# The final normalisation of an encoder trunk: half of its products given to GpSimd

## Chip, cores and metric

The kernel runs on one core of a Trainium2 chip. The metric is the time of one execution on the device in microseconds (us), as a median of several runs. Five engines work side by side on a core and meet by semaphores: TensorE (PE; PEld is its weight load), VectorE (DVE), ScalarE (ACT), GpSimd (POOL) and SyncE (SP), which here only issues transfers. An engine name with a q behind it is the engine's sequencer, which issues DMAs. The profile comes from one execution recorded by the hardware.

## What is computed

The reference is a trunk of two layers on 512 tokens of 1024 channels. Each layer adds a token mixer and then a gated feed-forward block to the residual stream x, and at the end stands an RMS norm with a gain for each channel:

```python
def rmsnorm(x, g):
    xf = x.astype(jnp.float32)
    y = xf * lax.rsqrt(jnp.mean(xf * xf, axis=-1, keepdims=True) + EPS)
    return (y * g.astype(jnp.float32)).astype(x.dtype)

def conv_ffn(h, w_up, conv_w, conv_b, w_down):
    u, v = jnp.split(h @ w_up, 2, axis=-1)
    u = causal_dwconv(u, conv_w, conv_b)
    return (jax.nn.gelu(u, approximate=False) * v) @ w_down

# in reference(), for each layer l:
        x = x + y                                   # the mixer
        x = x + conv_ffn(rmsnorm(x, ffn_norm[l]), ...)
    return rmsnorm(x, final_norm)
```

The change lies wholly in the last line, the final norm, and in what feeds it.

## The kernel before

The residual stream lies transposed in SBUF: channels on the 128 partitions, tokens along the row. `xall` holds eight tiles `x[0]` to `x[7]`, tile k with channels 128k to 128k+127 and 512 tokens; `x3` is the same memory seen as (partition, tile, token). All products with weights are done in three parts (high times high, high times low, low times high) to keep float32 accuracy. The page's L538 and L268 are these matmuls, L490 and L227 the splitting of weights into parts.

Order. In `ffn` (line 616) every step is put on a plan with a time worked out by hand (`at`), sorted, and traced in that order; `run_plan` (line 436) then holds TensorE, VectorE and ScalarE to it (`planned`, line 433). GpSimd and SP are not in that set: the framework orders what they issue, by what is ready and by the order in the program. DMAs that ScalarE issues stand in ScalarE's planned order.

The last down projection of the second layer (`halves_last`, lines 843 and 875 to 882) is cut in two halves of 256 tokens, so that the first half can be finished while TensorE works on the second. Each half is six groups of seven matmuls; in the second half a counter moves on behind each third of an `accumulate` (`tick`, line 252), and `after(n, fn)` (line 249) runs `fn` when the counter has moved n times. So the small matmuls of the first half's norm stand between the second half's groups.

For every tile j the plan calls `last(j)` (line 1463) when `x[j]` is final. For a whole tile (j from 0 to 6) it squares `x[j]` on ScalarE, adds the square to `acc` on VectorE (`square_acc`, line 288) and, for j up to 5, multiplies `x[j]` in place by the norm's gain on ScalarE (L1471). `x[7]` comes in halves: `last(7, 0)` and `last(7, 1)`. For a half of the tokens, these steps follow:

- the square of `x[7]`'s half on ScalarE (L1474);
- `one`: matmuls with a column of ones sum `acc` and the square over the channels, so that the sum for token t lies on partition t (L1481, bank `ss` of PSUM), and `rsqrt_small` (line 296) makes the root's reciprocal of 128x2 numbers: v = sum/width + eps on VectorE (L298), a first guess y on ScalarE straight from the sum (L300), and a Newton step t = y v, t = -t y / 2, y (t + 1.5) on VectorE (L304 to L306);
- `two`: `spread_small` (line 329) spreads the factor over all partitions with two matmuls against the identity (L332), into a bank `bc` of PSUM;
- `scale_out` (line 1501): for each pair of tiles k = 0, 2, 4, 6, VectorE multiplies the pair's half by the factor, read from PSUM. Pairs 0, 2 and 4 take one product of 128x512 (L1505); the pair 6 takes two operations of 128x256 (L1508), which also multiply by the gain. Then one DMA of 256 KB takes the pair's half to DRAM (L1511). In the first half all four are issued by SP, in the second pairs 2 and 6 by ScalarE.

The first half's `one` runs after two ticks and its `two` after four; its `scale_out` is traced only in `last(7, 1)`, behind the second half's residual sum (`add_x`, L814 and L815): pairs 0 and 2 first, pair 4 between the second half's guess y and its Newton step, pair 6 behind the step. The second half's `scale_out` ends the kernel.

Of the kernel before, what the change touches and what calls it, by code (L numbers as in the profile page):

```python
# [7 lines left out]
F32 = mybir.dt.float32  # L8
F32R = mybir.dt.float32r
I32 = mybir.dt.int32  # L10
AF = mybir.ActivationFunctionType
ALU = mybir.AluOpType

P = 128
T = 512
D = 1024
KD = D // P
# [7 lines left out]
EPS = 1e-6  # L25
# [48 lines left out]
def trunk_kernel(ctx, tc, xT, cols, w_ab, w_pool, w_abo, w_vg, w_qk, w_r, w_g2, w_go, w_up, w_dn, w_ds, outT):  # L74
    nc = tc.nc
    V, S, G, PE = nc.vector, nc.scalar, nc.gpsimd, nc.tensor
# [6 lines left out]
    sp = ctx.enter_context(tc.tile_pool(name="sp", bufs=2))  # L83
    ps = ctx.enter_context(tc.tile_pool(name="ps", bufs=8, space=bass.MemoryType.PSUM))

    def slot(dt=F32, name="s"):
        return big.tile([P, T], dt, tag="s", name=name)
# [17 lines left out]
    def bank(name="ps"):  # L105
        return ps.tile([P, T], F32, tag="ps", name=name)
# [3 lines left out]
    x = [xall[:, k * T : (k + 1) * T] for k in range(KD)]  # L110
# [4 lines left out]
    def col(name, i=0):  # L115
        c = COLS[name] + i
        return colt[:, c : c + 1]
# [45 lines left out]
    eps_t = cp.tile([P, 1], F32, tag="eps", name="eps_t")  # L163
# [85 lines left out]
    def after(n, fn):  # L249
        pending.append((done[0] + n, fn))  # L250
# [9 lines left out]
    def accumulate(out, wh, wl, ah, al, first=True, last=True, step=None, cut=0, loose=False):  # L260
        n = len(ah)
        if cut:
            accumulate(out, wh, wl, ah[:cut], al[:cut], first, False)
            accumulate(out, wh[:, cut:, :], wl[:, cut:, :], ah[cut:], al[cut:], False, last)
            return
        for i, (w, a) in enumerate(((wh, ah), (wh, al), (wl, ah))):
            for k in range(n):
                PE.matmul(  # L268
                    out, w[:, k, :], a[k], start=first and i == 0 and k == 0, stop=last and i == 2 and k == n - 1,
                    skip_group_check=loose,  # L270
                )
            if step:
                step()
# [14 lines left out]
    def square_acc(k, acc, ts=slice(0, T)):  # L288
        if k == 0 and ts.start == 0:
            S.activation(acc[:, ts], x[0][:, ts], AF.Square)  # L290
            return
        sq = slot(name="sq")
        S.activation(sq[:, ts], x[k][:, ts], AF.Square)
        V.tensor_tensor(acc[:, ts], acc[:, ts], sq[:, ts], ALU.add)

    def rsqrt_small(dst, ssum, n, width, between=None):
        v = sp.tile([P, n], F32, tag=f"v{n}", name="v")
        V.tensor_scalar(v, ssum, 1.0 / width, EPS, ALU.mult, ALU.add)  # L298
        y = sp.tile([P, n], F32, tag=f"y{n}", name="y")
        S.activation(y, ssum, AF.Abs_reciprocal_sqrt, bias=eps_t, scale=1.0 / width)  # L300
        if between:
            between()
        t = sp.tile([P, n], F32, tag=f"t{n}", name="t")
        V.tensor_tensor(t, y, v, ALU.mult)  # L304
        V.scalar_tensor_tensor(t, t, -0.5, y, ALU.mult, ALU.mult)
        V.scalar_tensor_tensor(dst, t, 1.5, y, ALU.add, ALU.mult)  # L306
# [22 lines left out]
    def spread_small(y, n):  # L329
        b = bank("bc")[:, : n * P]  # L330
        for c in range(n):
            PE.matmul(  # L332
                b[:, c * P : (c + 1) * P], y[:, c : c + 1].broadcast_to([P, P]), ident, start=True, stop=True
            )
        return b
# [32 lines left out]
    def scaled(o, rs, tag):  # L368
        u = slot(name=tag)
        V.tensor_tensor(u, o, rs, ALU.mult)  # L370
        return u
# [177 lines left out]
    def mix_out(name, gname, acc, lead, fetched):  # L549
# [6 lines left out]
        def part(n, ks, first, last):  # L556
            if first:
                o[n] = (bank(name), *ready.pop(0))
            out, h, lo = o[n]
            accumulate(out, h[:, ks, :], lo[:, ks, :], y_h[ks], y_l[ks], first, last, loose=True)  # L560
# [420 lines left out]
    for j in range(4):  # L981
# [7 lines left out]
        b = scaled(pb, rs, "v")  # L989
# [6 lines left out]
    total = []  # L996
# [272 lines left out]
    t = 0.0  # L1269
# [193 lines left out]
    def last(j, half=None):  # L1463
        if not squares:
            squares.append(slot(name="acc"))
        acc = squares[0]
        ts = slice(0, T) if half is None else slice(half * 256, half * 256 + 256)
        if half is None:
            square_acc(j, acc)
            if j < KD - 2:  # L1470
                S.activation(x[j], x[j], AF.Copy, scale=col("fin", j))  # L1471
            return
        sq = slot(name="sq")[:, :256]
        S.activation(sq, x[j][:, ts], AF.Square)  # L1474
        y2 = sp.tile([P, 2], F32, tag="y2", name="y2")

        def one(between=None):
            b = bank("ss")
            for i, t in enumerate((acc[:, ts], sq)):
                for c in range(2):  # L1480
                    PE.matmul(  # L1481
                        b[:, c : c + 1], t[:, c * P : (c + 1) * P], ones[:, 0:1],
                        start=i == 0 and c == 0, stop=i == 1, skip_group_check=True,
                    )
            rsqrt_small(y2, b[:, :2], 2, D, between)

        def two():
            return ts, spread_small(y2, 2)

        if half:  # L1490
            scale_out(*spread[0], (0, 2))
            one(lambda: scale_out(*spread[0], (4,)))
            scale_out(*spread[0], (6,))
            scale_out(*two(), range(0, KD, 2))
        else:
            after(2, one)
            after(4, lambda: spread.append(two()))

    spread = []

    def scale_out(ts, b, ks):
        for k in ks:
            o3 = x3[:, k : k + 2, ts]
            if k < KD - 2:
                V.tensor_tensor(o3, o3, b[:, None, :].broadcast_to([P, 2, 256]), ALU.mult)  # L1505
            else:
                for i in range(2):
                    V.scalar_tensor_tensor(  # L1508
                        x[k + i][:, ts], x[k + i][:, ts], col("fin", k + i), b, ALU.mult, ALU.mult
                    )  # L1510
            (nc.scalar if k % 4 and ts.start else nc.sync).dma_start(  # L1511
                outT[k * P : (k + 2) * P, ts].rearrange("(a p) t -> p a t", p=P), o3
            )
# [78 lines left out]
```

## Time and profile before

| | |
|---|---|
| median of 3 runs | 1006.32 us (1005.56 to 1007.13) |
| the profiled execution, time | 1006.93 us |
| its span | 1005.2 us, mean TensorE clock 0.997 |
| TensorE busy | 994.8 us, 99% of the span |
| VectorE, ScalarE, GpSimd busy | 851.2, 615.8, 81.3 us |
| HBM read, written | 145.35 MB, 2.10 MB |

How to read the profile's rows. In a timeline a row gives the start in us, the time in us, engine, line of the kernel, operation, output and inputs by tile names, shapes and how many; behind it in brackets, how long the engine was idle before and what released it. A group's row gives the total busy time and the mean in ns behind the bar. The chain is followed back from the last instruction, each step to what released it. A row of stretches gives for each engine its busy time and number of instructions, then TensorE's granted clock, the busy share of the 16 DMA engines and the rate in GB/s. DMA issues are not counted as busy time of the issuing engine. Times on GpSimd are rough.

### The profile page before, as it was taken

The numbers are of one execution on the slowest core, as the hardware profiler recorded it, in microseconds if no ns is written. First come the engines' busy times: TensorE is split into PE (matmuls) and PEld (weight loads), VectorE is DVE, ScalarE is ACT, GpSimd is POOL, SyncE is SP. The second block draws the span as 40 slices with busy tenths as digits, with TensorE's granted clock in tenths as the row PEclk, the third lists the DMA queues.
The fourth block names the chain that finished last, engine by engine and source line by source line (L and its number), as shares of the span: only waits on it lengthen the run. The fifth ranks groups of instructions, "written<-read, shape, count | busy, mean of one in ns | idle before, by whom it ended". The sixth has DMA issues, their size and how long they took to land.

```text
span 1005.2 us, 17757 instructions
## 1 busy us (share of the span) xinstructions
PE 994.8 (99%) x7070; PEld 927.9 (92%) x7070; DVE 851.2 (85%) x1241; ACT 615.8 (61%) x959; POOL 81.3 (8%) x105
## 2 busy tenths in 40 slices
PE   9999999999999999999999999999999999999996
PEld 7888889999999988899999998889999999988896
DVE  7886689999999997768768788889999999997775
ACT  6442467666766764445785677667766666754451
POOL 0000111111101000002000000111101101000000
PEclk9999999999999999999999999999999999999998
DMA  6523757787687454527326122676788777454522
GB/s 224 156 97 105 181 123 185 193 210 191 190 208 181 129 134 132 140 85 198 108 76 145 53 67 93 185 171 165 213 207 194 195 202 188 127 128 142 129 86 84
DMA packets 64083, 151.22 MB, mean 150 GB/s; under 512 B 5408, under 2 KB 8352, under 8 KB 64000
## 3 DMA queue, kind: packets, MB, share of 16 engines
q1 hardware_dynamic: 46640, 117.46, 37.8%
q0 software_dynamic: 16672, 31.99, 19.2%
q8 instruction: 55, 0.90, 0.3%
q10 hardware_dynamic: 688, 0.65, 0.2%
q14 instruction: 28, 0.23, 0.1%
HBM read 145.35 MB, written 2.10 MB: 147 GB/s over the span
## 4 chain that ended last, share of the span: by engine, by line
PE 91%; DVE 4%; DMA 2%; ACT 1%; issue 1%; DVEq 0%; ACTq 0%
PE stx L538 27%; PE styz L538 16%; PE dn L268 15%; PE r L1323 4%; PE abo L268 4%; PE go L268 4%; PE pc L268 2%; PE dn L538 2%; PE px L268 2%; PE pb L268 2%; DMA raw<-in_w_up 2%; PE stz L538 2%; PE vg L1111 1%; PE vg L1113 1%; PE vg L1112 1%; PE pu L268 1%
## 5 line engine op out<-in xcount | busy, mean ns | idle before, releaser
L490 DVE TENSOR_TENSOR lo<-raw,hi 128x1024 fp32r<-128x1024 f32 x112 | 136.7, 1221 | 14.1 <-ACT hi L484 13.8
L484 ACT ACTIVATE hi<-raw 128x1024 fp32r<-128x1024 f32 x112 | 117.8, 1057 | 33.2 <-DMA raw<-in_w_up 12.8
L227 DVE TENSOR_TENSOR lo<-raw,hi 128x1024 fp32r<-128x1024 f32 (+3 forms) x79 | 91.1, 1155 | 18.2 <-ACT hi L223 17.7
L466 POOL DMA_DIRECT2D s<-in_w_up x44 | 53.1, 1206 | 530.1 <-ACT yh L177 97.3
L223 ACT ACTIVATE hi<-raw 128x1024 fp32r<-128x1024 f32 (+3 forms) x79 | 78.7, 997 | 13.2 <-DMA raw<-in_w_ab 4.7
L359 DVE SCALAR_TENSOR_TENSOR cacc<-u,colt,cacc 128x511 f32<-128x511 f32 x96 | 71.5, 745 | 3.9 <-ACT cacc L356 3.8
L356 ACT ACTIVATE cacc<-u,colt 128x512 f32<-128x512 f32 x48 | 39.2, 817 | 49.5 <-DVE u L660 39.9
L490 DVE TENSOR_TENSOR lo<-s,hi 128x1024 fp32r<-128x1024 f32 x56 | 68.2, 1217 | 0.0
L538 PE MATMUL stx<-th,hi 128*128 128x256 f32 x384 | 59.4, 277 | 0.3 <-ACT kk L645 0.3
L484 ACT ACTIVATE hi<-s 128x1024 fp32r<-128x1024 f32 x56 | 59.0, 1053 | 0.7
L538 PE MATMUL stx<-th,lo 128*128 128x256 f32 x384 | 59.1, 276 | 0.0
L538 PE MATMUL stx<-tl,hi 128*128 128x256 f32 x384 | 59.1, 276 | 0.0
L538 PE MATMUL styz<-xl,hi 128*128 128x256 f32 x368 | 57.2, 277 | 0.3
L538 PE MATMUL styz<-xh,hi 128*128 128x256 f32 x368 | 56.9, 277 | 0.0
L538 PE MATMUL styz<-xh,lo 128*128 128x256 f32 x368 | 56.7, 276 | 0.0
L268 PE MATMUL dn<-mh,hi 128*128 128x512 f32 (+1 forms) x238 | 56.5, 377 | 0.0
L268 PE MATMUL dn<-mh,lo 128*128 128x512 f32 (+1 forms) x238 | 56.4, 376 | 0.0
L268 PE MATMUL dn<-ml,hi 128*128 128x512 f32 (+1 forms) x238 | 56.4, 376 | 0.0
L538 PEld LDWEIGHTS stx<-th,hi 128*128 128x128 f32 x384 | 50.7, 188 | 0.7 <-ACT kk L645 0.7
L538 PEld LDWEIGHTS stx<-tl,hi 128*128 128x128 f32 x384 | 50.7, 188 | 0.0
L538 PEld LDWEIGHTS stx<-th,lo 128*128 128x128 f32 x384 | 50.7, 188 | 0.0
L268 PEld LDWEIGHTS dn<-ml,hi 128*128 128x128 f32 x238 | 42.9, 188 | 8.2
(334 smaller groups left out, 2583.3 us busy)
## 6 DMA issues: line engine op xcount, KB each, us to landing
s<-in_w_up SPq DMA_DIRECT2D x44, 512.0 KB, 6.9
s<-in_w_up POOLq DMA_DIRECT2D x44, 512.0 KB, 7.3
raw<-in_w_up SPq DMA_DIRECT2D x44, 512.0 KB, 6.7
raw<-in_w_dn SPq DMA_DIRECT2D x32, 448.0 KB, 3.4
raw<-in_w_up SPq DMA_DIRECT2D x44, 256.0 KB, 3.6
raw<-in_w_ab SPq DMA_DIRECT2D x14, 512.0 KB, 3.6
raw<-in_w_abo SPq DMA_DIRECT2D x8, 512.0 KB, 3.6
s<-in_w_ds SPq DMA_DIRECT2D x8, 512.0 KB, 6.9
```

The source lines that it names most:

```text
L223: S.activation(parts[0], raw, AF.Copy)
L227: V.tensor_tensor(parts[1], raw, f32(parts[0]), ALU.subtract)
L268: PE.matmul(out, w[:, k, :], a[k], start=first and i == 0 and k == 0, stop=last and i == 2 and k == n - 1, skip_group_check=loose,)
L356: S.activation(acc[0], u, AF.Identity, bias=col(bname, j), scale=col(wname, 2 * nj + j))
L359: V.scalar_tensor_tensor(a, u[:, : T - i], col(wname, (2 - i) * nj + j), a, ALU.mult, ALU.add)
L466: G.dma_start(w["s31"].rearrange("p (a n) -> p a n", a=2), part, accum_op=ALU.add)
L484: S.activation(h, src(), AF.Copy)
L490: V.tensor_tensor(lo, src(), f32(h), ALU.subtract)
L538: PE.matmul(b[out][:, ts], wt[:, ks[k]], a[k], start=first and i == 0 and k == 0, stop=i == 2 and k == HK - 1, skip_group_check=True,)
L1111: PE.matmul(o[c][:, :n], xh[kk][:, cs], h[:, k, :], start=kk == 0, stop=False)
L1112: PE.matmul(o[c][:, :n], xl[kk][:, cs], h[:, k, :], start=False, stop=False)
L1323: PE.matmul(o, w[:, k, :], a[k], start=i == 0 and k == 0, stop=k == KD - 1 and i == 5, skip_group_check=True)
```

## The change

The final scaling is divided anew.

- The gain of `x[6]` is multiplied in ScalarE at once, as for tiles 0 to 5, and the gain of each half of `x[7]` by a ScalarE copy (`gain`). So the pair 6 needs no operation of its own, and every pair of a half is one product of 128x512.
[...]
- First half: after four ticks the factor is spread and copied, and GpSimd multiplies all four pairs.
- Second half: the factor is spread twice, into two banks. GpSimd takes pair 0 with a copy of the one, VectorE takes pairs 2, 4 and 6 from PSUM with the other. The DMAs keep their queues: SP for pair 0 and 4, ScalarE for 2 and 6.
- The root: `rsqrt_direct` does without v. It uses t = (sum + width eps) y, then t = -t y / (2 width), then y (t + 1.5): three operations on VectorE in place of four. The first reads the sum in PSUM.

```diff
@@ -1467,14 +1467,13 @@
             square_acc(j, acc)
-            if j < KD - 2:
-                S.activation(x[j], x[j], AF.Copy, scale=col("fin", j))
+            S.activation(x[j], x[j], AF.Copy, scale=col("fin", j))
             return
...
-        def one(between=None):
+        def one():
...
-            rsqrt_small(y2, b[:, :2], 2, D, between)
-
-        def two():
-            return ts, spread_small(y2, 2)
+            rsqrt_direct(y2, b[:, :2])
+
+        def rsqrt_direct(dst, total):
+            y = sp.tile([P, 2], F32, tag="y2b", name="y")
+            S.activation(y, total, AF.Abs_reciprocal_sqrt, bias=eps_t, scale=1.0 / D)
+            t = sp.tile([P, 2], F32, tag="t2", name="t")
+            V.scalar_tensor_tensor(t, total, D * EPS, y, ALU.add, ALU.mult)
+            V.scalar_tensor_tensor(t, t, -0.5 / D, y, ALU.mult, ALU.mult)
+            V.scalar_tensor_tensor(dst, t, 1.5, y, ALU.add, ALU.mult)
+
+        def gain():
+            S.activation(x[j][:, ts], x[j][:, ts], AF.Copy, scale=col("fin", j))
+
+        def copied():
+            gain()
+            factor = slot(name="bs")[:, :256]
+            S.activation(factor, spread_small(y2, 2), AF.Copy)
+            return factor
 
         if half:
-            scale_out(*spread[0], (0, 2))
-            one(lambda: scale_out(*spread[0], (4,)))
-            scale_out(*spread[0], (6,))
-            scale_out(*two(), range(0, KD, 2))
+            one()
+            factor = spread_small(y2, 2)
+            scale_out(ts, copied(), (0,), G)
+            scale_out(ts, factor, (2, 4, 6))
         else:
             after(2, one)
-            after(4, lambda: spread.append(two()))
-
-    spread = []
-
-    def scale_out(ts, b, ks):
+            after(4, lambda: scale_out(ts, copied(), range(0, KD, 2), G))
+
+    def scale_out(ts, b, ks, engine=V):
         for k in ks:
             o3 = x3[:, k : k + 2, ts]
-            if k < KD - 2:
-                V.tensor_tensor(o3, o3, b[:, None, :].broadcast_to([P, 2, 256]), ALU.mult)
-            else:
-                for i in range(2):
-                    V.scalar_tensor_tensor(
-                        x[k + i][:, ts], x[k + i][:, ts], col("fin", k + i), b, ALU.mult, ALU.mult
-                    )
+            engine.tensor_tensor(o3, o3, b[:, None, :].broadcast_to([P, 2, 256]), ALU.mult)
             (nc.scalar if k % 4 and ts.start else nc.sync).dma_start(
```

## The prediction, made before the changed kernel ran

> **What bounds the kernel now.** I read the page first, then the chain that ended last in order of time, then the stretches after the last big matmul, and last the timelines of VectorE, ScalarE, GpSimd and the issuing queues there.
>
> ```profile
> span 1005.2 us, 17757 instructions
> PE 994.8 (99%) x7070; PEld 927.9 (92%) x7070; DVE 851.2 (85%) x1241; ACT 615.8 (61%) x959; POOL 81.3 (8%) x105
> ```
>
> TensorE fills the span, so up to its last projection matmul it sets the time, and the change leaves its matmuls there alone. What can move is the tail. The chain, from there on:
>
> ```profile
> 993.29 1.65 PE dn L268 x14
> 994.95 0.02 issue
> 994.97 0.44 DVE dn L814
> 995.44 0.42 DVE xall L815
> 995.86 1.19 DVE xall L1505 x2
> 998.22 0.78 DVE xall L1508 x2
> 1000.31 0.60 DVE xall L1505
> 1000.91 0.78 DVE xall L1508 x2
> ```
>
> The big matmuls end at 994.95; 10.25 us follow, with VectorE on the chain until 1001.70 (1000.91 + 0.78, rounded). That looks like a tail bound by VectorE. The stretches say otherwise (columns: length; busy time of each engine with instructions; TensorE's clock; DMA share; GB/s):
>
> ```profile
> 997.00:997.50 0.50, 0.00 (x0) 0.00 (x0) 0.50 (x3) 0.24 (x1) 0.00 (x0) 1.00 0.15 53
> 997.50:999.50 2.00, 0.71 (x4) 0.52 (x4) 1.91 (x7) 0.03 (x1) 0.00 (x0) 1.00 1.03 343
> 1000.00:1003.60 3.60, 0.00 (x0) 0.00 (x0) 1.69 (x4) 0.00 (x0) 0.00 (x0) 0.50 1.01 342
> 1003.60:1003.80 0.20, 0.00 (x0) 0.00 (x0) 0.00 (x0) 0.00 (x0) 0.00 (x0) 0.50 0.79 277
> 1003.80:1004.00 0.20, 0.00 (x0) 0.00 (x0) 0.00 (x0) 0.00 (x0) 0.00 (x0) 0.50 0.14 41
> ```
> ```profile
> DMA packets 2176, 2.10 MB, mean 228 GB/s; under 512 B 128, under 2 KB 2176, under 8 KB 2176
> 996.48 0.40 SPq L1511 DMA_DIRECT2D out<-xall  x1
> 999.03 0.37 SPq L1511 DMA_DIRECT2D out<-xall  x1
> 1001.73 0.38 ACTq L1511 DMA_DIRECT2D out<-xall  x1
> ```
>
> From 1000.0 on the DMA engines are full (share 1.01, 342 GB/s) and stay so 2 us beyond VectorE's last result and the last issue (1001.73). The output is eight pieces of 256 KB; one takes 262144 B / 342 GB/s = 0.77 us. They run dry at about 1003.75, and 1.45 us later the span ends; I take those 1.45 us as fixed. So **the end is set by when the output can start to flow and by gaps in it**, not by VectorE alone. First data flows at about 997.4 (53 GB/s in 997.0 to 997.5 is 0.08 us at full rate), some 0.9 us after the first issue at 996.48; before the last first-half piece (999.03) the way was still full. Since later pieces may start a little sooner, I use 0.8 us as the lead of a transfer.
>
> **The change part by part.**
>
> 1. *x[6] gets its gain on ScalarE.* One copy of 0.73 us more, after the square at 985.23; ScalarE was then idle for 3.85 us. It costs nothing: with that idle time as cover, it ends at 986.6. Without it, the square at 989.71 would be late by up to 0.73 us.
>
> ```profile
> 977.70 0.73 ACT L1471 ACTIVATE xall<-xall,colt 128x512 f32<-128x512 f32 x1
> 985.23 0.63 ACT L293 ACTIVATE sq<-xall 128x512 f32<-128x512 f32 x1 [0.82 <-DVE xall L815]
> 989.71 0.42 ACT L1474 ACTIVATE sq<-xall 128x256 f32<-128x256 f32 x1 [3.85 <-DVE xall L815]
> 990.14 1.28 ACT L300 ACT_TABLE_LOAD   x1
> 991.44 0.26 ACT L300 ACTIVATE y<-ss,eps_t 128x2 f32<-128x2 f32 x1
> 991.73 0.16 DVE L304 TENSOR_TENSOR t<-y,v 128x2 f32<-128x2 f32 x1 [0.41 <-ACT y L300]
> 992.69 0.60 PE L332 MATMUL bc<-ident,y 128*128 128x128 f32 x4
> ```
>
> 2. *First half of the tokens.* The root without its first step saves nothing here: y at 991.44 comes 0.02 us behind a table load (990.14, 1.28 us), not behind v. The factor is spread over the partitions at 992.69 to 993.29 as before. New: ScalarE scales x[7] (half a row; 0.42 us by the square of that size), which fits between 991.70 and 993.29, and copies the factor out of PSUM (0.38 us by L798, below). GpSimd can start at about 993.80 (993.29 + 0.38, and 0.13 for two hand-overs, an estimate from the 0.03 to 0.06 us between engines in these rows, doubled for GpSimd). Before, VectorE took up this half only behind the second half's residual sum, at 995.86. Then four products of 128x512 on GpSimd.
>
> ```profile
> L798 ACT ACTIVATE kk<-stx 128x256 f32<-128x256 f32 x16 | 6.1, 380 | 34.2 <-PE stx L538 34.2
> L1015 POOL TENSOR_SCALAR_AFFINE_SELECT maskf<-maskf 128x512 f32<-128x512 f32 x1 | 1.2, 1187 | 0.0
> L1019 POOL MEMSET att<- 128x512 f32 x2 | 1.2, 582 | 0.0
> ```
>
> No product on GpSimd is in this trace. Bounds for one, g: not below the fill of a 128x512 tile, 0.58 us; not above twice the 1.19 us of the select, which reads one such tile and writes one, as the product reads two: 2.37 us. I take the nearest row, **g = 1.19 us**. [...]
>
> The four pieces are then ready at 994.99, 996.18, 997.37, 998.56, and their 3.08 us of transfer are over by about 1000.1, before the second half needs the way. Before, the first half's fourth piece left at 999.03.
>
> 3. *Second half, VectorE's share.* The four L1505/L1508 pieces of the first half leave VectorE. After the square (995.89 + 0.42) and the sum (matmuls to 996.97):
>
> ```profile
> 996.36 0.61 PE L1481 MATMUL ss<-ones,sq 128*128 128x1 f32 x4 [1.09 <-ACT sq L1474]
> 997.26 0.26 ACT L300 ACTIVATE y<-ss,eps_t 128x2 f32<-128x2 f32 x1 [0.95 <-DVE v L298]
> 997.87 0.16 DVE L305 SCALAR_TENSOR_TENSOR t<-t,y 128x2 f32<-128x2 f32 x1
> 998.06 0.16 DVE L306 SCALAR_TENSOR_TENSOR y<-t,y 128x2 f32<-128x2 f32 x1
> 998.28 0.71 PE L332 MATMUL bc<-ident,y 128*128 128x128 f32 x4 [1.31 <-DVE y L306]
> 999.03 1.88 DVE L1505 TENSOR_TENSOR xall<-xall,bc 128x512 f32<-128x512 f32 x3
> ```
>
> y waited for v (its row names it), so dropping v starts y at 997.00 instead of 997.26; then three small operations at 0.19 us spacing (998.06 - 997.87) start at 997.29, 997.48 and 997.67, and the factor is ready at 997.83 instead of 998.22: 0.39 us earlier, **if nothing holds VectorE up**. The spread takes 0.71 us plus 0.06 before and 0.04 behind; three products start 0.60 us apart (1.88 us for three, 0.68 the last).
>
> 4. *What GpSimd does to VectorE.* Here is the disputed term. The only place where a GpSimd operation that reads SBUF meets VectorE operations with two SBUF inputs:
>
> ```profile
> 473.31 1.19 POOL L1015 TENSOR_SCALAR_AFFINE_SELECT maskf<-maskf 128x512 f32<-128x512 f32 x1
> 473.92 0.85 DVE L388 TENSOR_TENSOR ta<-xg 128x256 f32<-128x256 f32 x1
> L388 DVE TENSOR_TENSOR ta<-xg x12: 415/419/854, 106.3 to 667.3; 128x256 f32<-128x256 f32 x12
> ```
>
> L388 takes 0.42 us in the median of 12; the one beside the select took 0.85 and ended 0.27 us behind it, as if it had run only from 474.35, 0.15 us before the select's recorded end. So it was held. The second and third of the new root's operations (t times y) have both inputs in SBUF too; the first, L814, L815 and VectorE's products read one input from PSUM, and I cost those at nothing, though no row shows them beside a GpSimd product: held as well, L815 (995.44) would move the second half by up to the 0.7 us that the second product then still runs. The second operation comes at 997.48, inside GpSimd's fourth product (997.37 to 998.56), and by that row would run at 998.41, the third at 998.60. The factor is then ready at 998.76: 0.93 us late, and 0.54 us later than before. Bounds of this wait: 0 (no hold), and one g for each of the two operations, 2.4 us, if GpSimd takes a fifth product in between; at g = 1.19 there is no fifth yet.
>
> [...]
>
> 5. *The last pieces.* With the wait: spread 998.82 to 999.53, VectorE's pieces ready at 1000.25, 1000.85 and 1001.45. The second spread for GpSimd ends near 1000.1, its copy at 1000.55, GpSimd's piece at 1001.8. Pieces two and six leave on ScalarE's queue, zero and four on SP's. SP's order isn't written by hand in the kernel. If four leaves ahead of zero, data flows from 1000.27 + 0.8 = 1001.07 without a gap and is out at 1001.07 + 3.08 = 1004.15: 0.40 us later than the 1003.75 of before. If SP waits for GpSimd's piece with four behind it, there is a gap until six flows at 1001.47 + 0.8 = 1002.27, and three pieces then end at 1004.58: 0.83 us later. Nothing in the trace decides between them; I take the middle.
>
> **Sum:** +0.6 us on the profiled execution's own 1006.93 us. That execution lies 0.6 us above the median of the three runs, 1006.32 (1005.56 to 1007.13), and I put the difference on the median: **1006.9 us**, no change that can be told: 0.2%, 2.0 us, is about what a measurement of this kernel can tell from no change.
>
> **The rivals.**
>
> *No hold on VectorE.* For it: the operations are 0.16 us long and only one row speaks for the hold. Against it: that row's size. Without the 0.93 us, flow starts at 1000.14 and ends at 1003.22 (0.53 us earlier), or at 1003.66 with the gap (0.09 earlier): mean -0.3, **1006.0 us**. More can't be had even so, since from VectorE's first second-half piece 3.08 us of transfer must pass. VectorE itself ends 1.15 us earlier than before, and the transfers give more than half of that back.
>
> *GpSimd is slow, and it becomes the end.* The mechanism: five products in a row on an engine whose product no row here shows. Its last piece is ready at 993.80 + 5g and is out at 993.80 + 5g + 0.82 + 0.77 = 995.39 + 5g. This is past 1003.75 from g = 1.67 us, and 2.0 us past it from g = 2.07. At the upper bound, 2.37, the data ends at 1007.24: +3.5, **1009.8 us**. For it: the select's 1.19 us for one input. Against it: part of those 1.19 us may itself be a wait, since a VectorE operation with two SBUF inputs (L227) ran until 474.00, and the same select on a quarter of the elements took 0.29 us.
>
> ```profile
> 472.77 1.23 DVE L227 TENSOR_TENSOR lo<-raw,hi 128x1024 fp32r<-128x1024 f32 x1 [1.49 <-ACT hi L223]
> L169 POOL TENSOR_SCALAR_AFFINE_SELECT ident<-ident 128x128 f32<-128x128 f32 x1 | 0.3, 287 | 0.0
> ```
>
> **How the numbers follow.** Forecast (VectorE held, g near 1.2): 0.55. No hold, or one that falls between products: 0.27. Slow GpSimd: 0.18, of which 0.10 with g over 2.07 or an unknown start of a like size. The first two lie within 2.0 us of the median (+0.8 to -0.5) with the runs' own scatter of 0.8 us; the third gives the slower side. So: faster 0.02, same 0.85, slower 0.13. The range takes the rival without a hold less the scatter (1006.0 - 0.8) and reaches up into the slow case to +2.3 us, which leaves its worst part out: 1005.2 to 1008.6.
>
> **What would show it.** Five GpSimd products, each near 1.2 us start to start; the second of VectorE's three small operations of the second half ending just behind GpSimd's fourth product (step 4 is wrong if it starts 0.03 us behind the first); first data at about 995.8; a DMA share of 1 from about 1001.1 to the end, with or without a gap before it (step 5); the end of the data 1.45 us before the span's. The forecast is wrong as a whole if products take over 1.7 us, if the first one starts well after 994, or if anything before 988 moves.

## The result and the profile after

| | before | after |
|---|---|---|
| median of 11 runs | 1006.43 us (1005.56 to 1007.44) | 1008.52 us (1006.94 to 1010.07) |
| ratio | 1 | 1.0019, 95% interval 1.0011 to 1.0027 |
| the profiled execution, time; span | 1006.93; 1005.2 us | 1007.74; 1006.0 us |
| big matmuls done, seen at the start of L814's second half | 994.97 | 994.16 |
| **tail**: from there to the end of the span | **10.23 us** | **11.84 us** |

The changed kernel is 2.1 us slower at the median, 0.2%; little, but the interval doesn't include 1. Up to the last big matmul nothing moved that can be told: the profiled execution of after was even 0.81 us ahead there, while its tail is 1.61 us longer. All distances below are therefore counted from the start of L814's second half, so that executions can be compared. The page gives the span to 0.1 us, so a tail is good to 0.05 us, and differences of less than 0.1 us between two tails say nothing.

The timeline of the changed kernel, all engines but for the weight loads; L1515 is the product by the factor, L1490 to L1492 are the three operations of the new root:

```profile
985.09 0.73 ACT L1470 ACTIVATE xall<-xall,colt 128x512 f32<-128x512 f32 x1
988.90 0.42 ACT L1473 ACTIVATE sq<-xall 128x256 f32<-128x256 f32 x1 [3.09 <-DVE xall L815]
...
993.00 4.95 POOL L1515 TENSOR_TENSOR xall<-xall,bs 128x512 f32<-128x512 f32 x4 [49.18 <-ACT bs L1500]
...
994.16 0.43 DVE L814 TENSOR_TENSOR dn<-dn,rs 128x256 f32<-128x256 f32 x1 [2.69 <-PE dn L268]
...
994.63 0.42 DVE L815 TENSOR_TENSOR xall<-dn,xall 128x256 f32<-128x256 f32 x1
...
996.50 0.16 DVE L1490 SCALAR_TENSOR_TENSOR t<-ss,y 128x2 f32<-128x2 f32 x1 [1.44 <-ACT y L1488]
996.69 1.28 DVE L1491 SCALAR_TENSOR_TENSOR t<-t,y 128x2 f32<-128x2 f32 x1
998.00 0.16 DVE L1492 SCALAR_TENSOR_TENSOR y<-t,y 128x2 f32<-128x2 f32 x1
998.22 2.08 PE L332 MATMUL bc<-ident,y 128*128 128x128 f32 x8 [2.06 <-DVE y L1492]
999.48 1.88 DVE L1515 TENSOR_TENSOR xall<-xall,bc 128x512 f32<-128x512 f32 x3 [1.32 <-PE bc L332]
1000.34 0.38 ACT L1500 ACTIVATE bs<-bc 128x256 f32<-128x256 f32 x1 [3.48 <-PE bc L332]
...
1000.80 1.27 POOL L1515 TENSOR_TENSOR xall<-xall,bs 128x512 f32<-128x512 f32 x1 [2.85 <-ACT bs L1500]
```

Read L1491 first: 128x2 numbers, 1.28 us where its neighbours of the same shape take 0.16. It ends at 997.97, 0.02 us behind GpSimd's fourth product (993.00 + 4.95). In the four other runs below that have t in SBUF and GpSimd on the first half (e1, e4, e6, e9) it takes 1.27 to 1.30 us and ends 0.01 to 0.02 us behind that product too. This hold stands in the operation's own busy time, not in the idle time in brackets; whoever looks for waits alone doesn't see it. Then read the spread: eight matmuls in 2.08 us, where four took 0.71 before.

GpSimd's products, all five as a group (shortest, median and longest in ns), and the issues of the output:

```profile
L1515 POOL TENSOR_TENSOR xall<-xall,bs x5: 1252/1255/1280, 993.0 to 1000.8; 128x512 f32<-128x512 f32 x5
994.31 0.40 SPq L1516 DMA_DIRECT2D out<-xall  x1
...
1000.34 1.44 ACTq L1516 DMA_DIRECT2D out<-xall  x2
1002.09 0.91 SPq L1516 DMA_DIRECT2D out<-xall  x2
```

The stretches of the changed kernel (the last three columns are TensorE's clock, DMA share, GB/s):

```profile
995.00:996.00 1.00, 0.44 (x4) 0.44 (x4) 0.06 (x1) 0.42 (x1) 1.00 (x2) 1.00 0.75 255
996.00:996.50 0.50, 0.17 (x2) 0.08 (x1) 0.00 (x1) 0.30 (x2) 0.50 (x1) 0.54 0.10 31
998.00:1000.00 2.00, 1.78 (x8) 1.78 (x8) 0.68 (x2) 0.00 (x0) 0.00 (x0) 0.50 0.60 205
1000.00:1001.00 1.00, 0.30 (x2) 0.00 (x1) 1.00 (x3) 0.38 (x1) 0.20 (x1) 0.50 0.00 0
1001.00:1002.00 1.00, 0.00 (x0) 0.00 (x0) 0.36 (x1) 0.00 (x0) 1.00 (x1) 0.50 0.74 249
1002.00:1002.50 0.50, 0.00 (x0) 0.00 (x0) 0.00 (x0) 0.00 (x0) 0.06 (x1) 0.50 0.44 150
1002.50:1004.50 2.00, 0.00 (x0) 0.00 (x0) 0.00 (x0) 0.00 (x0) 0.00 (x0) 0.50 1.02 344
1004.50:1005.00 0.50, 0.00 (x0) 0.00 (x0) 0.00 (x0) 0.00 (x0) 0.00 (x0) 0.50 0.23 76
```

Two things are to be seen. TensorE's clock falls to 0.5 within 996.0 to 996.5, ahead of the spread; in the profile before, it was still 1.00 up to 999.5 and fell at 999.9. And the DMA engines, full from 1000.0 on before (share 1.01), stand still for the whole of 1000.0 to 1001.0, and have another gap in 1002.0 to 1002.5 (share 0.44). The first half left early, as planned, and the second half's first data flow only at 1001.27: the work taken from VectorE made a hole, not time.

### The profile page after: what moved, and what is told of

Its sections match the earlier page's. It is cut to its first block, busy times and chain, and to the rows that moved or that the text cites. A ratio compares the mean times of both kernels' runs of the same rounds, so it can differ in the third digit from the quotient of the medians.

```text
span 1006.0 us, 17766 instructions
## 1 busy us (share of the span) xinstructions
PE 995.4 (99%) x7074; PEld 928.8 (92%) x7074; DVE 849.1 (84%) x1232; ACT 618.2 (61%) x964; POOL 87.4 (9%) x110
## 4 chain that ended last, share of the span: by engine, by line
PE 96%; DMA 1%; DVE 1%; POOL 0%; issue 0%; ACT 0%; POOLq 0%; SPq 0%; ACTq 0%
PE stx L538 29%; PE styz L538 18%; PE dn L268 15%; PE r L1323 4%; PE abo L268 4%; PE go L268 4%; PE pc L268 2%; PE dn L538 2%; PE pb L268 2%; PE px L268 2%; PE stz L538 2%; PE vg L1111 1%; PE vg L1113 1%; PE vg L1112 1%; PE pu L902 1%; PE pu L268 1%
## 5 line engine op out<-in xcount | busy, mean ns | idle before, releaser
L538 PE MATMUL stx<-th,hi 128*128 128x256 f32 x384 | 59.3, 276 | 0.2 <-ACT kk L645 0.2
L538 PE MATMUL stx<-th,lo 128*128 128x256 f32 x384 | 59.2, 276 | 0.0
L538 PE MATMUL stx<-tl,hi 128*128 128x256 f32 x384 | 59.1, 276 | 0.0
L538 PE MATMUL styz<-xl,hi 128*128 128x256 f32 x368 | 57.2, 277 | 0.3
L538 PE MATMUL styz<-xh,hi 128*128 128x256 f32 x368 | 56.9, 277 | 0.0
L538 PE MATMUL styz<-xh,lo 128*128 128x256 f32 x368 | 56.7, 276 | 0.0
L538 PEld LDWEIGHTS stx<-th,hi 128*128 128x128 f32 x384 | 50.7, 188 | 0.4 <-ACT kk L645 0.4
L538 PEld LDWEIGHTS stx<-th,lo 128*128 128x128 f32 x384 | 50.7, 188 | 0.0
L538 PEld LDWEIGHTS stx<-tl,hi 128*128 128x128 f32 x384 | 50.7, 188 | 0.0
L268 PEld LDWEIGHTS dn<-mh,lo 128*128 128x128 f32 x238 | 42.9, 188 | 8.2
```

The lines of the kernel that those rows point to most:

```text
L268: PE.matmul(out, w[:, k, :], a[k], start=first and i == 0 and k == 0, stop=last and i == 2 and k == n - 1, skip_group_check=loose,)
L538: PE.matmul(b[out][:, ts], wt[:, ks[k]], a[k], start=first and i == 0 and k == 0, stop=i == 2 and k == HK - 1, skip_group_check=True,)
```

## Experiments

The theory behind them: the longer tail has three causes, the hold of L1491 (some 1.1 us), TensorE's clock (0.5 us) and pair 4 behind pair 0 on SP (0.4 us). Its rivals are given with each. All are edits of the changed kernel; none leaves anything out. "Clock up" says whether TensorE's clock was still 1 when the first spread ran.

| kernel | clock up | first second-half product | tail | median | ratio to before (95%) |
|---|---|---|---|---|---|
| before | yes | 4.06 | 10.23 | 1006.43 | 1 |
| after | no | 5.32 | 11.84 | 1008.52 | 1.0019 (1.0011 to 1.0027) |
| e2: t in PSUM | no | 4.21 | 10.73 | 1034.27 | 1.0268 (1.0255 to 1.0281) |
| e2b: the same, layout kept | no | 4.21 | 10.82 | 1006.95 | 0.9994 (0.9978 to 1.0009) |
| e1: SP order, not changed | yes | 4.80 | 11.36 | 1008.48 | 1.0012 (1.0003 to 1.0021) |
| e9: SP order forced | no | 5.31 | 11.66 | 1007.66 | 1.0010 (1.0000 to 1.0019) |
| e6: TensorE kept busy | yes | 4.83 | 11.39 | 1007.52 | 1.0005 (0.9996 to 1.0013) |
| e4: second half VectorE's | yes | 4.82 | 10.89 | 1008.06 | 1.0018 (1.0003 to 1.0032) |
| e5: no GpSimd | yes | 3.95 | 10.05 | 1007.22 | 0.9993 (0.9978 to 1.0007) |
| e7: e2b and e4 | yes | 3.70 | 9.98 | 1006.59 | 0.9992 (0.9974 to 1.0010) |
| e8: e7 and filling | yes | 3.70 | 9.99 | 1006.52 | 0.9988 (0.9973 to 1.0003) |
| e11: VectorE in its idle time | yes | 3.68 | 9.85 | 1006.35 | 0.9996 (0.9987 to 1.0005) |
| e12: e11 and filling | yes | 3.69 | 9.77 | 1006.03 | 0.9995 (0.9986 to 1.0004) |

Ratios are to runs of the kernel before on the same chip, whose medians lay between 1006.43 and 1007.20 us. The median of e2 is one of four runs, the others are of 11 or 12. The tails come from one profile each, but they repeat well (e1 and e6, e7 and e8) where the same things are at work; most of the medians can't be told apart.

### e2 and e2b: the hold

```diff
-            rsqrt_direct(y2, b[:, :2])
+            rsqrt_direct(y2, b[:, :2], b[:, 2:4])
-        def rsqrt_direct(dst, total):
+        def rsqrt_direct(dst, total, t):
...
-            t = sp.tile([P, 2], F32, tag="t2", name="t")
+            sp.tile([P, 2], F32, tag="t2", name="spare")     # e2b alone
```

> The changed kernel, but t of the root lies in PSUM (columns 2 and 3 of the sum's bank) instead of SBUF, so that each of the three small VectorE operations reads one input from SBUF and one from PSUM; nothing is left out. Tail here is the span's end less the start of L814's second half: 10.23 us before, 11.84 us in the changed kernel. Theory A (the second operation was held 1.1 us because both its inputs lay in SBUF while a GpSimd product read SBUF): it takes 0.16 to 0.2 us instead of 1.28 with GpSimd's fourth product still running, the factor is ready 1.1 us earlier and the tail is near 10.8 us; median about 1.0 us below the changed kernel. Rival B (any small VectorE operation beside a GpSimd product is held, wherever its inputs lie): it still takes about 1.2 us, tail 11.8 us.

> As e2_t_in_psum (t of the root in PSUM), but the two 128x2 places in SBUF that t had are still taken, unused, so that every tile lies where it lies in the changed kernel. Theory A (the 26 us more of e2_t_in_psum come from the shifted addresses of what is allocated behind, not from the root; the root's gain is the missing hold): matmuls back at a mean of 276 ns (stx, styz), second small operation 0.17 us, tail 10.7 us as in e2_t_in_psum and 1.1 us less than the changed kernel's 11.84, median about 1.1 us below it. Rival (t in PSUM itself slows the program): median again over 1030 us.

VectorE and GpSimd in e2b:

```profile
995.58 0.43 DVE L814 TENSOR_TENSOR dn<-dn,rs 128x256 f32<-128x256 f32 x1 [2.67 <-PE dn L268]
...
997.91 0.17 DVE L1490 SCALAR_TENSOR_TENSOR ss<-ss,y 128x2 f32<-128x2 f32 x1 [1.44 <-ACT y L1488]
998.12 0.17 DVE L1491 SCALAR_TENSOR_TENSOR ss<-ss,y 128x2 f32<-128x2 f32 x1
998.32 0.16 DVE L1492 SCALAR_TENSOR_TENSOR y<-ss,y 128x2 f32<-128x2 f32 x1
...
994.42 4.95 POOL L1515 TENSOR_TENSOR xall<-xall,bs 128x512 f32<-128x512 f32 x4 [49.59 <-ACT bs L1500]
```

L1491 runs at 998.12 in the midst of GpSimd's products (to 999.37) and takes 0.17 us. Only the place of t changed, which L1491 reads and writes. So theory A holds and rival B falls: beside GpSimd's products L1491 took 1.28 us with both its inputs in SBUF and 0.17 us with one of them in PSUM, so it isn't held by GpSimd's work as such. The tail shrinks by 1.02 us (11.84 to 10.82), with the clock fallen in both, and the ratio falls from 1.0019 to 0.9994, with intervals that don't meet. That t as an output was the cause is out as well: in the changed kernel L1490 writes it to SBUF beside GpSimd in 0.16 us. And without GpSimd on the first half (e5, e11, e12) the same operation with both inputs in SBUF takes 0.16 us. In the changed kernel L814, L815 and L1490, each with one input from PSUM, ran beside GpSimd in their usual 0.43, 0.42 and 0.16 us. The prediction had costed these three at nothing without a row that shows it; these rows now do.

e2 also gave a surprise: 1034 us with the good tail. The group of the costliest matmuls in the changed kernel, and then in e2:

```profile
L538 PE MATMUL stx<-tl,hi 128*128 128x256 f32 x384 | 59.1, 276 | 0.0
```
```profile
L538 PE MATMUL stx<-tl,hi 128*128 128x256 f32 x384 | 61.6, 282 | 0.0
```

With two 128x2 places less in one pool, the largest groups of L538's matmuls take 282 to 283 ns instead of 276 to 277, and TensorE is busy for 1023.0 us against 996.2 in e2b. With the places kept (e2b), the matmuls are back at 276 to 277 ns and the time at 1007 us. The two kernels differ in nothing but these places, and the kernel before ran alike on the two chips they ran on (1006.99 and 1007.20 us), so the places make the difference. That it comes about by the addresses of what is allocated behind them is argued, not shown, and which tile has to lie where wasn't tried.

### e1 and e9: the order on SP

```diff
-            scale_out(ts, copied(), (0,), G)
+            scale_out(ts, copied(), (0,), G, out=False)
             scale_out(ts, factor, (2, 4, 6))
+            scale_out(ts, None, (0,), None)            # the DMA alone; in e9 inside
+                                                       # "with tc.issue_after(issued[4]):"
```

> The changed kernel, but in the second half the DMA of pair 0 (GpSimd's) is issued behind that of pair 4 on SP; nothing is left out. Theory A (part of the loss is that pair 4, ready at 1000.7, stands on SP's queue behind pair 0, ready at 1002.1, so that the transfers have a gap): no gap from the first second-half piece on, data out 0.4 us earlier, tail 11.4 us. Rival (the hold and the clock alone set the end): tail 11.8 us, as in the changed kernel.

> What e1_sp_order meant to do and did not: there SP still issued pair 0 (ready at 1002.9) ahead of pair 4 (ready at 1001.6). Here an edge makes pair 0's DMA follow pair 4's on SP; nothing is left out. Tail is the span's end less the start of L814's second half: 11.84 us in the changed kernel with TensorE's clock fallen before the spread, 11.36 and 11.39 with the clock still up. Theory A (pair 4 behind pair 0 costs 0.4 us by a gap of the transfers): pair 4 issued within 0.05 us of its product's end, no idle time of the DMA engines from the first second-half data on, tail 11.4 us with the clock fallen, 10.9 with the clock up. Rival (the gap is there anyway, since the pieces are ready too far apart): tail 11.8 and 11.4.

The issues on SP in e1, then in e9:

```profile
1002.91 0.37 SPq L1520 DMA_DIRECT2D out<-xall  x1
1003.38 0.45 SPq L1520 DMA_DIRECT2D out<-xall  x1
```
```profile
1001.22 0.40 ACTq L1523 DMA_DIRECT2D out<-xall  x1
1001.67 0.37 SPq L1523 DMA_DIRECT2D out<-xall  x1
1002.27 0.38 ACTq L1523 DMA_DIRECT2D out<-xall  x1
1002.96 0.37 SPq L1523 DMA_DIRECT2D out<-xall  x1
```

e1 failed as an experiment: written behind the others, pair 0's DMA is still the first on SP, and pair 4, ready at 1001.62, waits until 1003.38. The framework orders SP by its own idea of what is ready; that it took GpSimd for faster than it is would explain this, but isn't shown. The run serves as a repeat of the changed kernel with the clock up. In e9 pair 4 leaves at once, and the gap is gone: data flows from 1002.15 to 1005.22 without a break. But this is worth 0.18 us of the tail (0.24 by the unrounded spans in the packed traces), not 0.4. The gap it closed was 0.28 us long, shorter than I had worked out.

### e6: TensorE's clock

```diff
+        def fill(n):
+            spare = bank("warm") if half and n else None
+            for i in range(n if half else 0):
+                PE.matmul(spare[:, :P], ones, ones, start=True, stop=True)
...
             for i, t in enumerate((acc[:, ts], sq)):
+                fill(3 * i)
...
             one()
+            fill(6)
```

> The changed kernel, with 3 matmuls of no use on TensorE ahead of the square's sum and 6 ahead of the factor's spread in the second half, to keep TensorE busy; the output is the same. Theory A (part of the loss is that TensorE's granted clock fell to 0.5 at 996.0, ahead of the two spreads, so that eight matmuls took 2.08 us where four took 0.71 before): the clock stays at 1.0 until the spreads are through, VectorE's first second-half product starts 0.5 us earlier, GpSimd's last 1.1 us earlier, tail 11.3 us. Rival (the clock falls whatever TensorE does there, or the spread is hidden): first product at the same distance from L814 (5.3 us), tail 11.8 us; if the filling delays the spread, over 12.

The stretches of e6 around the two spreads:

```profile
996.00:999.00 3.00, 2.14 (x17) 1.86 (x16) 1.59 (x3) 1.01 (x3) 2.82 (x3) 1.00 0.68 229
999.00:1000.50 1.50, 1.16 (x8) 0.97 (x8) 0.70 (x3) 0.22 (x1) 0.00 (x0) 1.00 0.71 236
```

The clock stays at 1.00 (third column from the end) through both spreads, which take 1.16 us instead of 2.08. The tail is 0.45 us shorter, GpSimd's last product starts 5.73 us after L814 instead of 6.64. The runs lie closer together too: 1007.34 to 1008.63 us, against 1006.94 to 1010.07 in the changed kernel; whether that is the clock stays open, since filling narrowed nothing in e8 and e12 below. Without the filling the clock falls at different moments: 1.9 to 2.9 us after L814 in four profiles (after, e2, e2b, e9) and 3.8 to 4.9 us in six (before, e1, e4, e5, e7, e11), with no edit that explains the groups.

The clock records of the packed traces say more. In all 13 the clock is recorded as full for one stretch: 989.87 us in the changed kernel, 993.28 in eight others, 996.69 in the three with filling and 1020.59 in e2, which runs 27 us longer. The longer ones are one, two and nine times 3.413 us above the shortest ((1020.59 - 989.87) / 9), and each length is a whole number of such steps: 290, 291, 292 and 299. So in these 13 the clock fell at such a step each time, and where the steps lie against L814 differs from one execution to the next. What has to happen within a step isn't shown: TensorE was busy for 2.31 us in the step at whose end the clock fell in the changed kernel (992.63 to 996.04), and for 2.31 us in the one before the last in the kernel before (993.07 to 996.48), at whose end it stayed up.

### e4, e5 and e7: GpSimd's share

```diff
-            scale_out(ts, copied(), (0,), G)           # e4 and e7
-            scale_out(ts, factor, (2, 4, 6))
+            gain()
+            scale_out(ts, factor, range(0, KD, 2))
```

In e5 both halves are VectorE's, in the order of the kernel before, with the new root and the gains on ScalarE:

```diff
-            one()
-            factor = spread_small(y2, 2)
-            scale_out(ts, copied(), (0,), G)
-            scale_out(ts, factor, (2, 4, 6))
+            scale_out(*spread[0], (0, 2))
+            one(lambda: scale_out(*spread[0], (4,)))
+            scale_out(*spread[0], (6,))
+            scale_out(*two(), range(0, KD, 2))
...
-            after(4, lambda: scale_out(ts, copied(), range(0, KD, 2), G))
+            after(4, lambda: spread.append(two()))
```

> The changed kernel, but the second half is all VectorE's (one spread, no copy, four products in order 0, 2, 4, 6); GpSimd keeps the first half. Nothing is left out. Theory A (GpSimd's share of the second half gains nothing, since its piece is the last one ready, and the order on SP costs 0.4 us): the hold of 1.1 us stays, products end 2.5 us after the first starts, transfers without a gap, tail 11.3 us, 0.5 us below the changed kernel. Rival (GpSimd's share does relieve VectorE): the last product ends 0.6 us later than the 7.2 us after L814 and the tail is 12.4 us.

> The part without GpSimd: gains of x[6] and x[7] on ScalarE, root without v, every pair one VectorE product, the first half's products in the order of the kernel before (two ahead of the sum, one behind y, one behind the root). Nothing is left out. Theory A (the loss comes with GpSimd; the transfers bound the end): first data as before, eight transfers in a row, the last pair ready 0.6 to 0.8 us earlier than before, tail 9.9 to 10.2 us against 10.23, median within 0.4 us of the kernel before. Rival (the gain copies or the direct root lose something): tail over 10.5 us.

> e2b and e4 together: GpSimd has the first half only, t in PSUM, the second half all VectorE's. Theory A (hold and GpSimd's share of the second half are separate losses): no hold, first second-half product 4.2 us after L814 if the clock has fallen by then and 3.7 if not, then four transfers in a row: tail 9.8 to 10.3 us, at or just below the kernel before. Rival (GpSimd in the first half still delays something else): tail over 10.6 us.

VectorE in e4 and then in e5:

```profile
996.43 1.28 DVE L1491 SCALAR_TENSOR_TENSOR t<-t,y 128x2 f32<-128x2 f32 x1
997.75 0.16 DVE L1492 SCALAR_TENSOR_TENSOR y<-t,y 128x2 f32<-128x2 f32 x1
998.73 2.48 DVE L1515 TENSOR_TENSOR xall<-xall,bc 128x512 f32<-128x512 f32 x4 [0.82 <-PE bc L332]
```
```profile
994.75 0.43 DVE L814 TENSOR_TENSOR dn<-dn,rs 128x256 f32<-128x256 f32 x1 [2.69 <-PE dn L268]
...
998.70 2.48 DVE L1517 TENSOR_TENSOR xall<-xall,bc 128x512 f32<-128x512 f32 x4 [0.21 <-PE bc L332]
```

e4: four products on VectorE end 7.30 us after L814 (998.73 + 2.48 less 993.91). GpSimd's one piece ended at 7.91 in the changed kernel, but with the clock up, as in e4, it was hardly later: 7.34 in e1 (1001.62 + 1.26 less 995.54). Against e1, which has the same hold and clock, the tail is 0.47 us shorter (the expected 11.3 us counts from the changed kernel with its fallen clock), and most of that lies on the way out. The second half's data start 6.45 us after L814 in e4 and flow without a break; in e1 they start at 6.56, behind the factor's copy on ScalarE's queue, and stand still for 0.32 us. So GpSimd's share of the second half is a loss by itself: it brings the copy and the order on SP, and relieves a VectorE that keeps ahead of the transfers anyway (0.60 against 0.77 us a piece).

e5: without GpSimd, root and gains are worth 0.18 us of the tail, as theory A had it, though the last pair is ready only 0.30 us earlier, not 0.6 to 0.8. The gain has another source. In the kernel before, the DMA engines had a hole of 0.24 us ahead of the first half's fourth piece (share 0.52), in a stretch that the prediction's rows leave out:

```profile
999.50:1000.00 0.50, 0.00 (x0) 0.00 (x0) 0.50 (x2) 0.00 (x0) 0.00 (x0) 0.90 0.52 180
```

In e5 that piece is issued 3.81 us after L814 instead of 4.06, and the share of the same stretch is 0.98.

e7 puts GpSimd back into the first half, without the hold: 9.98 against 10.05, a difference at the limit of what the tails resolve. GpSimd's work earned no more here. In e7 the way out is busy with the first half when the second is ready: GpSimd's fourth product is issued at 998.53, the second half's first at 999.13. From e4 to e7, with the clock up at the spread in both, the hold is worth 0.91 us.

### e8, e11 and e12: what would be better

e8 adds the filling to e7 (3 and 3 matmuls). e11 has no GpSimd: VectorE multiplies pairs 0 and 2 of the first half when the factor is there, and 4 and 6 while the second half's sum and guess run; e12 adds the filling.

```diff
+        def early():
+            spread.append(two())
+            scale_out(*spread[0], (0, 2))
...
         if half:
+            scale_out(*spread[0], (4, 6))
             one()
+            scale_out(*two(), range(0, KD, 2))
         else:
             after(2, one)
+            after(4, early)
```

> e7 with 3 matmuls of no use ahead of the square's sum and 3 ahead of the factor's spread in the second half, so that TensorE's clock stays up. Theory A (the clock's fall before the spread is the third loss, and its moment changes from run to run): first second-half product 3.7 us after L814, tail 9.7 us, 0.5 us below the kernel before, and a scatter of the runs under 1.5 us. Rival (the clock matters little): as e7, with its scatter.

> A version without GpSimd meant to beat both: VectorE multiplies pairs 0 and 2 of the first half as soon as the factor is spread (it was idle for 2.7 us ahead of L814's second half), pairs 4 and 6 behind L815 while the second half's sum and guess run (1.4 us idle), and the whole second half at the end; root and gains as in the change. Nothing is left out. Theory A (only the moment from which the second half's data can flow sets the end): L814 not delayed, first second-half product 3.7 us after L814, four transfers in a row, tail 9.7 us against 10.23 before and 9.98 to 10.05 in e5, e7 and e8; median 0.5 us below the kernel before. Rival (the pairs in the idle time hold up L814 or the root): tail 10.2 us or more.

> e11 with 3 matmuls of no use ahead of the square's sum and 3 ahead of the factor's spread in the second half. Theory A (the moment at which the clock falls makes the runs scatter): tail 9.7 us, as e11 with the clock up, and a narrower scatter of the runs; median at or up to 0.3 us below e11. Rival (the fall of the clock does not reach the end here): no difference from e11.

VectorE in e11:

```profile
992.81 1.28 DVE L1518 TENSOR_TENSOR xall<-xall,bc 128x512 f32<-128x512 f32 x2 [1.05 <-PE bc L332]
994.45 0.43 DVE L814 TENSOR_TENSOR dn<-dn,rs 128x256 f32<-128x256 f32 x1 [0.35 <-PE dn L268]
994.91 0.42 DVE L815 TENSOR_TENSOR xall<-dn,xall 128x256 f32<-128x256 f32 x1
995.25 1.27 DVE L1518 TENSOR_TENSOR xall<-xall,bc 128x512 f32<-128x512 f32 x2
996.78 0.16 DVE L1490 SCALAR_TENSOR_TENSOR t<-ss,y 128x2 f32<-128x2 f32 x1 [0.25 <-ACT y L1488]
```

The two pairs ahead of L814 end 0.35 us before it can start, the other two 0.25 us before y is there: all four fit into time in which VectorE waited. The tails are the shortest, 9.85 and 9.77 us, against the 9.7 that theory A gave and 10.23 before. In the medians this is 0.3 and 0.6 us under the kernel before, and both intervals include no change. In e8 the filling brought nothing (9.99 against 9.98, the clock being up in the profile of e7 too), and its runs, 1005.55 to 1008.02, scatter more than e7's, of which all but one (1014.52) lie within 1006.25 to 1006.90. Those of e12 (1005.22 to 1007.31) scatter as those of e11 (1005.71 to 1007.68). That part of the expectation fell. So e12 beats the changed kernel and has a shorter tail than the kernel before; that it is faster than the latter is not shown by the times.

## Why the prediction was right and where it was not

The forecast was "no change that can be told", 1006.9 us; it came out 1.6 us above that, and the slowdown of 0.2% can just be told. The range, up to 1008.6, held by 0.08 us, and its upper end had been set for a slow GpSimd, which did not come: that it held is in part luck. The mechanism of step 4, which turned the forecast from a gain into a small loss, was right; the sum was too small. Step by step, in us after L814:

- *Steps 1 and 2, x[6] and the first half: right.* x[6]'s copy ended 3.09 us before the next square. GpSimd started at 993.00, which is the forecast 993.80 in an execution 0.81 us ahead; a product took 1.23 us from start to start (three spacings in 4.95 - 1.26), against 1.19. The rival of a slow GpSimd is out.
- *Step 3, the root: right.* y came at 2.04, forecast 2.03.
- *Step 4, the hold: right, and somewhat short.* The second operation waited 1.12 us, not 0.93. It ended at 997.97 and takes 0.16 us, so it ran from 997.81, 0.14 us ahead of the product's recorded end, as L388 had it (0.15). What was short is g: four products took 4.95 us, not 4.76, so the fourth ended 0.20 us later than forecast. The third operation ended at 4.00 instead of 3.79: +0.21. The rival without a hold is out.
- *Step 5, the spread: the step that failed.* I took its time, 0.71 us, over from the profile before, and with it a TensorE at full clock. Between the start of the spread and the first product lay 1.26 us, not 0.75: +0.51. The prediction shows the row in which the clock stands at 1.00 until 999.5; I read it as a fact about the kernel, and it is one about the moment. e6 shows the cause, worth 0.45 us. But this term belongs to the execution as much as to the change: with the clock up in both (e1 against before) the tail grew by 1.13 us, and with a fall 1.9 us after L814 the spread of the kernel before, 3.3 to 4.0 us after it, would have met half the clock as well. How much of it is in the medians isn't known.
- *Step 5, the issue:* the first transfer of the second half left 0.16 us late, since on ScalarE's queue the factor's copy stands ahead of the DMA; in the trace both begin at 1000.34, 0.18 us behind the product's end (999.48 + 0.68). I hadn't counted what stands there: +0.16. And data came 0.93 us after the issue, not 0.8: +0.13. The prediction's own row had 0.9, and I had taken off 0.1 without a row that shows it.
- *Step 5, SP's order:* pair 0 ahead of pair 4, the worse of my two cases; the gap was 0.28 us against 0.43, with 0.21 in the middle value: +0.07. From the last data to the span's end it took 1.37, not 1.45: -0.08, of which the rounding of the spans can be up to 0.05.

These add up to 0.21 + 0.51 + 0.16 + 0.13 + 0.07 - 0.08 = 1.00 us, and with the 0.6 of the forecast to the 1.61 that the tail grew. The measured medians are 2.1 us apart, with an interval of 1.1 to 2.7; what lies between 1.6 and 2.1 is not settled, nor need it be more than the scatter.

That the way was still full before the first half's last piece was misread (see e5); the sum doesn't rest on it.

That the start of the second half's data and the gaps in the transfers set the end was right, and it is why the change couldn't win: with the hold away and the second half left to VectorE, GpSimd gains about 0.1 us at most over VectorE alone (e7 against e5).

## What to carry to other kernels

Before moving work to another engine, ask what sends the results away: here the transfers already followed one another without a gap (share 1.01 from 1000.0 on before), so only an earlier start of the last part could help, and GpSimd's help was worth about 0.1 us at most while the hold cost 0.9 to 1.0. Keep small operations on the critical path that read two tiles in SBUF from running beside GpSimd's products (1.28 us where its neighbours took 0.16), or put one input in PSUM, which freed the one here (0.17 us). And a duration taken over from the profile holds for its moment: the spread, at full clock in the profile before (0.71 us for four matmuls), ran at half the clock in the changed kernel's (2.08 us for eight, against 1.16 in e6).

## What the runs showed of the hardware

- A VectorE operation of 128x2 with both inputs in SBUF took 1.28 us beside a GpSimd product and 0.17 us with one input in PSUM; the hold shows as busy time.
- A GpSimd product of 128x512 with the factor in SBUF, read twice, took 1.25 to 1.28 us, 1.23 from start to start; VectorE's, with the factor in PSUM, took 0.68.
- TensorE's clock fell 1.9 to 4.9 us after L814, differently in profiles of the same order of work; in all 13 traces the length of its full stretch, 989.87 to 1020.59 us, was a whole number of steps of 3.413 us, and with nine matmuls of no use it stayed up until both spreads were done.
- Two 128x2 places less in SBUF cost 27 us (1034.3 against 1007.0 us), with L538's matmuls at 282 instead of 276 ns.
